# Two hybrid decoder layers on one core: the weight sums of the feed-forward block queued behind the first block's factors, the even half of each up block finished first, and three products opened together in each group

## The chip, the core and the metric

The kernel runs on one core of one Trainium2 chip. The metric is the device time of one execution in microseconds (us), as the median of several runs. The engines are named as the profile names them: PE is TensorE (matmuls and transposes), DVE is VectorE, ACT is ScalarE, POOL is GpSimd, SP is SyncE, which here only issues transfers. Each engine works through its own queue of instructions in order, and waits there for what other engines owe it.

## The reference, cut to what matters

Two decoder layers over 512 tokens with a model width of 1024, all in float32. Around the change only the second half of a layer counts:

```python
x = layer_norm(DN_ALPHA * x + mix, ln1_g, ln1_b)      # after attention
g, u = jnp.split(x @ w_gu, 2, axis=-1)                # w_gu: 1024 x 5632
ffn = (jax.nn.silu(g) * u) @ w_down                   # w_down: 2816 x 1024
ple = (p_i @ w_pp) * jax.nn.sigmoid(x @ w_pg)
return layer_norm(DN_ALPHA * x + ffn + ple, ln2_g, ln2_b)
```

The first half of a layer (a combined input projection, a sliding-window attention, a sparse attention with a top-k per query, an output projection) stays as it is.

## The kernel before, in words

Every float32 matmul is done as three matmuls on a rounded high part and a rest (`mm3`, lines 307 to 311: high by high at line 309, then the two mixed products at 310 and 311). So each weight tile is split: ACT copies the rounded high part (lines 254 and 274) and POOL subtracts to get the rest (lines 255 and 275). The split tiles live in the pool `wsp`, which has five buffers; `w_rel` gives a buffer back and lets the next tile be split. Raw weights arrive by SP's queue in `wst` (three buffers) or, for `w_down`, in `slot` tiles.

The hidden width of 2816 is worked through in eleven *blocks* of 256 columns, and the blocks in *groups* of two: (0, 1), (2, 3), (4, 5), (6, 7), (8, 9), and block 10 alone.

For a block, `gate_up` (line 824) multiplies the transposed activations `fh`/`fl` (all 512 tokens) by four weight tiles: first the two *gate* accumulators, then the two *up* accumulators, one for the first 128 columns of the block (the even half) and one for the last 128 (the odd half), 24 matmuls in each of the four. Every accumulator is one of the eight PSUM buffers with the tag `bank`. In the kernel before, the even and the odd accumulator take turns after every three matmuls. Then ACT applies SiLU to the gates, and DVE multiplies them by the ups (line 849).

For the groups of two blocks, the product with `w_down` is a seven-product (Strassen-Winograd) form over token halves and block halves. It needs sums on both sides:

- `factors` (line 859) makes the sums of the activations on DVE (lines 866, 867, 869, 870) and splits each into high part (ACT, line 855) and rest (DVE, line 856).
- The *weight sums* combine four quarters of `w_down` on DVE: lines 243, 244 and 245 make t1, t2 and t3, each in two instructions of 128x512, and line 259 makes t4 in two more. All operands are in SBUF. In the kernel before, t1 to t3 are written down when the group's raw weights come up in the queue of splits (`w_split`, entry "raw"), and t4 when the first quarter has been split.
- `down` (line 877) does the seven products into six accumulators and adds each result into the residual stream with DVE (`res_out`, line 768, or 770 on the first touch). Some accumulators go on accumulating after they have been added once, so PE can write such a bank again only when DVE has read it.

Nobody writes the order of the instructions by hand here: the kernel is written as one program, and a scheduler with a model of times orders the instructions of each engine, keeping their dependencies. So what is written next to what decides the order only in part, and the order after the change is shown below from the built programs.

After the eleven blocks the layer multiplies the activations by `w_pg` and `p` by `w_pp`, half of their weights split into `slot` tiles by ACT and DVE (lines 268 and 269), and ends with the second layer norm. Before the feed-forward part stands the first layer norm (`ln_sums`, lines 388 to 397) and the transposition of its result (`to_features`, line 399: eight PE transposes at line 405 for each of four token blocks, copied by ACT at 407 and split by DVE at 408).

## Time and profile before

| | |
|---|---|
| median of three runs | 1326.42 us (1325.2 to 1326.89) |
| the profiled execution | 1327.37 us, of which the span from first to last instruction is 1325.6 us |
| PE busy | 1255.6 us, 95% |
| weight loads of PE | 1078.0 us, 81% |
| DVE busy | 854.6 us, 64% |
| POOL busy | 674.4 us, 51% |
| ACT busy | 564.4 us, 43% |
| mean granted TensorE clock | 0.98 |

Times within the profile are counted from the first instruction. The feed-forward parts, with what follows them in the layer, take from 241 to 656 us and from 888 us to the end. In a row of the profile, a number in square brackets is the time for which the engine stood idle just before the instruction, with the engine and the tile that ended the idle time; "x3" means that three equal instructions are put together. PE starts a 128x512 matmul every 0.227 us when nothing holds it, though one such matmul lasts 0.39 us, because they overlap.

### The profile page before, as it was taken

How to read it: one execution, taken by the hardware profiler on the slowest of the kernel's cores; microseconds unless marked ns; L12 is line 12 of the kernel's file. 1: busy time of each engine (PE TensorE's matmuls, PEld its weight loads, DVE VectorE, ACT ScalarE, POOL GpSimd, SP SyncE). 2: the span in 40 equal slices, each digit the busy share in tenths (PEclk: the TensorE clock that was granted, in tenths of full speed). 3: DMA queues.
4: the chain of work that ended last, by engine and by line, in shares of the span. 5: the costliest groups of instructions: out<-in, count | busy, mean ns of one | idle time of the engine just before them, and what ended most of it. 6: DMA issues, size and time to landing. Idle time of an engine off the chain costs nothing.

```text
span 1325.6 us, 18330 instructions
## 1 busy us (share of the span) xinstructions
PE 1255.6 (95%) x6632; PEld 1078.0 (81%) x6632; DVE 854.6 (64%) x1846; ACT 564.4 (43%) x1196; POOL 674.4 (51%) x477
## 2 busy tenths in 40 slices
PE   6799999799999999999998999999999999999996
PEld 4799889687878787887897998978878787878785
DVE  8899965838273737345678998675646464544266
ACT  3657765343333333333336577742424242333220
POOL 7465432356475747572055544323665656656422
PEclk9799999899999999999998999999999999999999
DMA  5133211333233323134032313103241414130421
GB/s 167 49 96 96 80 49 33 96 112 95 80 96 95 103 88 112 48 96 148 1 81 79 113 33 112 48 18 110 96 133 58 143 48 143 52 123 27 121 76 48
DMA packets 89123, 112.77 MB, mean 85 GB/s; under 512 B 5444, under 2 KB 65860, under 8 KB 89032
## 3 DMA queue, kind: packets, MB, share of 16 engines
q1 hardware_dynamic: 88360, 111.58, 27.3%
q8 instruction: 52, 0.85, 0.3%
q14 instruction: 39, 0.32, 0.1%
q10 hardware_dynamic: 672, 0.03, 0.0%
HBM read 109.49 MB, written 2.10 MB: 84 GB/s over the span
## 4 chain that ended last, share of the span: by engine, by line
PE 68%; DVE 24%; issue 3%; ACT 2%; POOL 1%; DMA 1%; DVEq 0%; SPq 0%; POOLq 0%; ACTq 0%
PE bank L309 21%; PE bank L311 20%; PE bank L310 20%; DVE x L768 3%; DVE t2k L243 2%; DVE slot L245 2%; PE bank L649 2%; DVE t2k L469 2%; PE bank L693 2%; DVE m L624 2%; DVE work L625 2%; DVE slot L856 1%; POOL wsp L275 1%; DVE t2k L244 1%; DVE t2k L467 1%
## 5 line engine op out<-in xcount | busy, mean ns | idle before, releaser
L275 POOL TENSOR_TENSOR wsp<-wst,wsp 128x1024 fp32r<-128x1024 f32 (+2 forms) x148 | 364.7, 2478 | 270.0 <-ACT wsp L274 269.7
L310 PE MATMUL bank<-fl,wsp 128*128 128x512 f32 (+1 forms) x768 | 286.8, 374 | 2.0 <-DVE fl L408 2.0
L309 PE MATMUL bank<-fh,wsp 128*128 128x512 f32 (+1 forms) x768 | 285.3, 374 | 1.0 <-ACT fh L407 1.0
L311 PE MATMUL bank<-fh,wsp 128*128 128x512 f32 (+1 forms) x768 | 284.9, 373 | 0.0
L274 ACT CAST wsp<-wst 128x1024 fp32r<-128x1024 f32 (+2 forms) x148 | 151.9, 1032 | 212.2 <-PE bank L311 143.2
L849 DVE TENSOR_TENSOR t2k<-bank,t2k 128x512 f32<-128x512 f32 x44 | 30.0, 691 | 284.3 <-PE bank L311 283.9
L255 POOL TENSOR_TENSOR wsp<-slot,wsp 128x512 fp32r<-128x512 f32 x100 | 135.9, 1383 | 95.6 <-ACT wsp L254 95.6
L309 PE MATMUL bank<-wsp,slot 128*128 128x512 f32 x392 | 156.7, 400 | 15.5 <-DVE x L768 12.1
L310 PEld LDWEIGHTS bank<-fl,wsp 128*128 128x128 f32 x768 | 146.5, 191 | 27.5 <-DVE fl L408 2.4
L309 PEld LDWEIGHTS bank<-fh,wsp 128*128 128x128 f32 x768 | 145.3, 191 | 26.6 <-ACT fh L407 1.9
L311 PEld LDWEIGHTS bank<-fh,wsp 128*128 128x128 f32 x768 | 146.4, 191 | 25.2
L309 PE MATMUL bank<-wsp,fh 128*128 128x256 f32 (+3 forms) x512 | 166.2, 326 | 0.6 <-ACT fh L407 0.2
L311 PE MATMUL bank<-wsp,fl 128*128 128x256 f32 (+3 forms) x512 | 164.9, 323 | 1.6 <-DVE fl L408 1.6
L310 PE MATMUL bank<-wsp,fh 128*128 128x256 f32 (+3 forms) x512 | 164.8, 322 | 0.2 <-POOL wsp L275 0.2
L310 PE MATMUL bank<-wsp,slot 128*128 128x512 f32 x392 | 154.1, 393 | 0.0
L311 PE MATMUL bank<-wsp,slot 128*128 128x512 f32 x392 | 144.9, 393 | 0.0
L768 DVE TENSOR_TENSOR x<-bank,x 128x512 f32<-128x512 f32 x140 | 89.5, 681 | 40.8 <-PE bank L311 40.8
L309 PEld LDWEIGHTS bank<-wsp,fh 128*128 128x128 f32 x512 | 98.4, 193 | 7.4 <-ACT fh L407 0.9
L311 PEld LDWEIGHTS bank<-wsp,fl 128*128 128x128 f32 x512 | 98.3, 192 | 7.2 <-DVE fl L408 2.2
L309 PEld LDWEIGHTS bank<-wsp,slot 128*128 128x128 f32 x392 | 74.3, 190 | 36.6 <-DVE x L768 18.0
L310 PEld LDWEIGHTS bank<-wsp,fh 128*128 128x128 f32 x512 | 98.5, 192 | 6.0 <-POOL wsp L275 0.5
L254 ACT CAST wsp<-slot 128x512 fp32r<-128x512 f32 x100 | 57.1, 618 | 92.1 <-PE bank L311 56.4
(166 smaller groups left out, 2184.2 us busy)
## 6 DMA issues: line engine op xcount, KB each, us to landing
wst<-in_w_gu_dram SPq DMA_DIRECT2D x88, 512.0 KB, 3.5
slot<-in_w_down_dram SPq DMA_DIRECT2D x80, 256.0 KB, 2.8
wst<-in_w_in_dram SPq DMA_DIRECT2D x16, 512.0 KB, 3.7
wst<-in_w_o_dram SPq DMA_DIRECT2D x16, 512.0 KB, 3.7
wst<-in_w_pg_dram SPq DMA_DIRECT2D x16, 512.0 KB, 3.7
wst<-in_w_in_dram SPq DMA_DIRECT2D x8, 256.0 KB, 2.8
lng<-in_ln_g_dram SPq DMA_DIRECT2D x4, 512.0 KB, 4.8
lnb<-in_ln_b_dram SPq DMA_DIRECT2D x4, 512.0 KB, 6.2
```

The source lines that it names most:

```text
L243: V.tensor_tensor(q["t1"][j], q["12"][j], q["11"][j], OP.subtract)
L245: V.tensor_tensor(q["12"][j], q["22"][j], q["12"][j], OP.subtract)
L254: A.copy(w[:, 0, j], src[j])
L255: G.tensor_tensor(w[:, 1, j], src[j], w[:, 0, j], OP.subtract)
L274: A.copy(w[:, 0, :a * n], st[:, :a * n])
L275: G.tensor_tensor(w[:, 1, :a * n], st[:, :a * n], w[:, 0, :a * n], OP.subtract)
L309: PE.matmul(o, sh, mh, start=start, stop=False, skip_group_check=again)
L310: PE.matmul(o, sh, ml, start=False, stop=False, skip_group_check=again)
L311: PE.matmul(o, sl, mh, start=False, stop=stop, skip_group_check=again)
L469: V.tensor_tensor(t1.rearrange("p n (u i) -> p n u i", u=2), t1.rearrange("p n (u i) -> p n u i", u=2), t2.rearrange("p n (u i) -> p n u i ...
L768: V.tensor_tensor(xt[t][:, c], ps, xt[t][:, c], OP.add)
L849: V.tensor_tensor(a, ps[1, f], a, OP.mult)
```

## The change

Four things are rewritten:

1. **The weight sums move.** t1, t2 and t3 are no longer made when the raw quarters come up in the queue of splits, but in a function of their own, `w_sums`, which the driver calls after the first block of the group. `tc.issue_after` tells the scheduler to place them on DVE after a given instruction, here the last split of that block's factors. t4 is tied to the same place.
2. **The up half of a block.** The even accumulator gets all its 24 matmuls first, then the odd one. SiLU, the multiplication and the even part of the factors follow as soon as their half is done. The third weight tile of a block is given back 12 matmuls later than before, since the odd half still needs it.
3. **The factors.** They are made in two steps, one for each half, and the sum for the first split product (s1) is split by itself ahead of the others.
4. **The products.** Three products with six accumulators are opened at the start of a group, instead of two with four accumulators, and each result is added as soon as its product is done.

The amount of arithmetic on PE, ACT and POOL stays the same, except that one split of 128x512 in the factors becomes two of 128x256. The transfers and their order on SP are the same.

```diff
@@ -237,16 +237,9 @@
     def w_split(i):
 
         if wq[i][0] == "raw":
-            q = quarter
-            q["t1"], q["t2"] = ([t2k() for _ in range(2)] for _ in range(2))
-            for j in range(2):
-                V.tensor_tensor(q["t1"][j], q["12"][j], q["11"][j], OP.subtract)
-                V.tensor_tensor(q["t2"][j], q["22"][j], q["t1"][j], OP.subtract)
-                V.tensor_tensor(q["12"][j], q["22"][j], q["12"][j], OP.subtract)
-            q["t3"] = q.pop("12")
             return
         if wq[i][0] == "op":
-            src = quarter.pop(wq[i][1])
+            src = quarter[wq[i][1]]
             wpos["room"] -= 1
...
@@ -255,8 +248,10 @@
                 G.tensor_tensor(w[:, 1, j], src[j], w[:, 0, j], OP.subtract)
             if wq[i][1] == "11":
                 quarter["t4"] = src
-                for j in range(2):
-                    V.tensor_tensor(src[j], quarter["21"][j], quarter["t2"][j], OP.subtract)
+            if wq[i][1] == "t1":
+                with tc.issue_after(quarter["after"]):
+                    for t4, b, t2 in zip(quarter["t4"], quarter["21"], quarter["t2"]):
+                        V.tensor_tensor(t4, b, t2, OP.subtract)
...
@@ -275,6 +270,18 @@
...
+
+    def w_sums(after):
+
+        q = quarter
+        q["after"] = after
+        q["t1"], q["t2"] = ([t2k() for _ in range(2)] for _ in range(2))
+        with tc.issue_after(after):
+            for j in range(2):
+                V.tensor_tensor(q["t1"][j], q["12"][j], q["11"][j], OP.subtract)
+                V.tensor_tensor(q["t2"][j], q["22"][j], q["t1"][j], OP.subtract)
+                V.tensor_tensor(q["12"][j], q["22"][j], q["12"][j], OP.subtract)
+        q["t3"] = q["12"]
 
     def w_pump():
         while True:
@@ -821,58 +828,79 @@
         load_gb(("2", l), ln2_g, ln2_b, l * D)
 
 
-        def gate_up(first):
+        def gate_up(first, made):
+
             ps = {}
             ws = take(4)
+
+            def product(j, f, k, r):
+                wh, wl = (ws[2 * j + k // 4][s][k % 4][:, f * 128:(f + 1) * 128] for s in range(2))
+                mm3(ps[j, f][:, r], wh, wl, fh[:, k, r], fl[:, k, r], k == 0, k == KT - 1)
+
+            def finish(f):
+                a = t2k()
+                A.activation(a, ps[0, f], AF.Silu)
+                V.tensor_tensor(a, ps[1, f], a, OP.mult)
+                made(f, a)
+
             if first:
                 to_features(0)
                 to_features(1)
-            for r in ((0, 256), (256, 512)) if first else ((0, 512),):
                 for j in range(2):
-                    for f in range(2):
-                        if (j, f) not in ps:
-                            ps[j, f] = acc()
+                    ps[j, 0], ps[j, 1] = acc(), acc()
                     for k in range(KT):
-                        wh, wl = (ws[2 * j + k // 4][s][k % 4] for s in range(2))
                         for f in range(2):
-                            fs = slice(f * 128, (f + 1) * 128)
-                            mm3(ps[j, f][:, r[0]:r[1]], wh[:, fs], wl[:, fs],
-                                fh[:, k, r[0]:r[1]], fl[:, k, r[0]:r[1]], k == 0, k == KT - 1)
-                        if r[1] == 512 and k % 4 == 3:
-                            w_rel()
-                    if first and r[0] == 0:
-                        to_features(2 + j)
-            raw = []
+                            product(j, f, k, slice(0, 256))
+                    to_features(2 + j)
+            r = slice(256, 512) if first else slice(0, 512)
             for f in range(2):
-                a = t2k()
-                A.activation(a, ps[0, f], AF.Silu)
-                V.tensor_tensor(a, ps[1, f], a, OP.mult)
-                raw.append(a)
-            return raw
+                if (0, f) not in ps:
+                    ps[0, f] = acc()
+            for k in range(KT):
+                for f in range(2):
+                    product(0, f, k, r)
+                if k % 4 == 3:
+                    w_rel()
+            for f in range(2):
+                if (1, f) not in ps:
+                    ps[1, f] = acc()
+                for k in range(KT):
+                    product(1, f, k, r)
+                    if f == 1 and k % 4 == 3:
+                        w_rel()
+                finish(f)
 
         def parts(src, pair=None):
             h = pair or [slot()[:, :src.shape[1]] for _ in range(2)]
             A.copy(h[0], src)
-            V.tensor_tensor(h[1], src, h[0], OP.subtract)
-            return h
-
-        def factors(raw):
+            end = V.tensor_tensor(h[1], src, h[0], OP.subtract)
+            return h, end.ins
+
+        def factors(r):
 
             lo, hi = slice(0, 256), slice(256, 512)
-            e, o = raw
-            q1, q2 = t2k(), t2k()
-            a11 = slot()
-            r = {"11": parts(e[:, lo], [a11[:, lo], a11[:, hi]])}
-            V.tensor_tensor(q1[:, lo], e[:, hi], o[:, hi], OP.add)
-            V.tensor_tensor(q1[:, hi], q1[:, lo], e[:, lo], OP.subtract)
-            s12 = parts(q1)
-            V.tensor_tensor(q2[:, lo], e[:, lo], e[:, hi], OP.subtract)
-            V.tensor_tensor(q2[:, hi], o[:, lo], q1[:, hi], OP.subtract)
-            odd, s34 = parts(o), parts(q2)
-            for name, src, c in (("s1", s12, lo), ("s2", s12, hi), ("12", odd, lo), ("22", odd, hi),
-                                 ("s3", s34, lo), ("s4", s34, hi)):
-                r[name] = [p[:, c] for p in src]
-            return r
+
+            def made(f, a):
+                r[f] = a
+                if f == 0:
+                    a11 = slot()
+                    r["11"], _ = parts(a[:, lo], [a11[:, lo], a11[:, hi]])
+                    r["q"] = t2k()
+                    V.tensor_tensor(r["q"][:, lo], a[:, lo], a[:, hi], OP.subtract)
+                    return
+                e, o = r.pop(0), r.pop(1)
+                q1, q2 = t2k(), r.pop("q")
+                s12 = [slot(), slot()]
+                V.tensor_tensor(q1[:, lo], e[:, hi], o[:, hi], OP.add)
+                r["s1"], _ = parts(q1[:, lo], [p[:, lo] for p in s12])
+                odd, _ = parts(o)
+                V.tensor_tensor(q1[:, hi], q1[:, lo], e[:, lo], OP.subtract)
+                r["s2"], _ = parts(q1[:, hi], [p[:, hi] for p in s12])
+                V.tensor_tensor(q2[:, hi], o[:, lo], q1[:, hi], OP.subtract)
+                s34, r["end"] = parts(q2)
+                for name, src, c in (("12", odd, lo), ("22", odd, hi), ("s3", s34, lo), ("s4", s34, hi)):
+                    r[name] = [p[:, c] for p in src]
+            return made
 
         def down(hs, first):
 
@@ -891,33 +919,30 @@
                         sh, sl = hs[f][left]
                         mm3(ps[u], sh[:, c], sl[:, c], w[0][f], w[1][f], new and f == 0, stop and f == 1, True)
 
-            pa, pc = [acc(), acc()], [acc(), acc()]
-            w1, w5 = take(2)
+            pa, pc, pb = ([acc(), acc()] for _ in range(3))
+            three = tuple(zip(("11", "s1", "12"), take(3), (pa, pc, pb), ((0, 0), (1, 1), (0, 0))))
             for f in range(2):
-                product("11", w1, pa, (f,), True, True)
-                if f == 1:
-                    w_rel()
-                product("s1", w5, pc, (f,), True, True)
-            w_rel()
-            add(0, 0, pa)
-            add(1, 1, pc)
-            pb = [acc(), acc()]
-            for left, ps, new, out in (("12", pb, True, (0, 0)), ("s2", pa, False, (0, 1)),
-                                       ("s4", pc, False, (0, 1)), ("s3", pa, False, (1, 1)),
-                                       ("22", pa, False, (1, 0))):
+                for left, w, ps, out in three:
+                    product(left, w, ps, (f,), True, True)
+                    if f == 1:
+                        w_rel()
+                        add(*out, ps)
+            for left, ps, out in (("s2", pa, (0, 1)), ("s4", pc, (0, 1)), ("s3", pa, (1, 1)), ("22", pa, (1, 0))):
                 w = w_take()
-                product(left, w, ps, (0, 1), new, True)
+                product(left, w, ps, (0, 1), False, True)
                 w_rel()
                 add(*out, ps)
 
         for gi, fs in enumerate(GROUPS):
             hs = []
             for f in fs:
-                raw = gate_up(f == 0)
                 if len(fs) == 2:
-                    hs.append(factors(raw))
+                    hs.append({})
+                    gate_up(f == 0, factors(hs[-1]))
+                    if f == fs[0]:
+                        w_sums(hs[0]["end"])
                 else:
-                    hs += [parts(a) for a in raw]
+                    gate_up(False, lambda f, a: hs.append(parts(a)[0]))
                 if gi == 1 and f == fs[0]:
                     pT = {}
                     for k in range(2):
```

What this does to the order of DVE at the end of a group, here the third one of the first layer. `x_85` to `x_88` are the four token blocks of the residual stream, `bank` is an accumulator, `slot` a quarter of `w_down` and `t2k` a sum. Before:

```order
L768 TENSOR_TENSOR x_87<-bank,x_87 128x512
L243 TENSOR_TENSOR t2k<-slot 128x512
L768 TENSOR_TENSOR x_88<-bank,x_88 128x512
L768 TENSOR_TENSOR x_85<-bank,x_85 128x512
L768 TENSOR_TENSOR x_86<-bank,x_86 128x512
L768 TENSOR_TENSOR x_85<-bank,x_85 128x512
L244 TENSOR_TENSOR t2k<-slot,t2k 128x512
L245 TENSOR_TENSOR slot<-slot 128x512
L243 TENSOR_TENSOR t2k<-slot 128x512
L768 TENSOR_TENSOR x_86<-bank,x_86 128x512
L768 TENSOR_TENSOR x_85<-bank,x_85 128x512
L244 TENSOR_TENSOR t2k<-slot,t2k 128x512
```

After, the same adds (now line 775) follow each other, with the group's last factor splits (line 876) ahead of them:

```order
L876 TENSOR_TENSOR slot<-t2k,slot 128x512
L775 TENSOR_TENSOR x_85<-bank,x_85 128x512
L775 TENSOR_TENSOR x_86<-bank,x_86 128x512
L775 TENSOR_TENSOR x_87<-bank,x_87 128x512
L775 TENSOR_TENSOR x_88<-bank,x_88 128x512
L775 TENSOR_TENSOR x_85<-bank,x_85 128x512
L775 TENSOR_TENSOR x_86<-bank,x_86 128x512
L775 TENSOR_TENSOR x_85<-bank,x_85 128x512
```

The sums of the next group have left this place. They now stand between the factors of a group's first block and the multiplication (line 843) of its second block:

```order
L876 TENSOR_TENSOR slot<-t2k,slot 128x512
L281 TENSOR_TENSOR t2k<-slot 128x512
L282 TENSOR_TENSOR t2k<-slot,t2k 128x512
L283 TENSOR_TENSOR slot<-slot 128x512
L281 TENSOR_TENSOR t2k<-slot 128x512
L254 TENSOR_TENSOR slot<-slot,t2k 128x512
L282 TENSOR_TENSOR t2k<-slot,t2k 128x512
L283 TENSOR_TENSOR slot<-slot 128x512
L254 TENSOR_TENSOR slot<-slot,t2k 128x512
L843 TENSOR_TENSOR t2k<-bank,t2k 128x512
```

All eight sums of a group stand there one after the other, ahead of everything that the second block needs of DVE.

On PE, the up half of block 10 (its two accumulators have the numbers 5716 and 5717 before) takes turns before:

```order
L309 MATMUL bank_5716<-fh_83,wsp_5611 128x512
L310 MATMUL bank_5716<-fl_84,wsp_5611 128x512
L311 MATMUL bank_5716<-fh_83,wsp_5611 128x512
L309 MATMUL bank_5717<-fh_83,wsp_5611 128x512
L310 MATMUL bank_5717<-fl_84,wsp_5611 128x512
L311 MATMUL bank_5717<-fh_83,wsp_5611 128x512
```

After, the even accumulator (5736) has its 24 matmuls over both weight tiles before the odd one (5768) begins:

```order
L316 MATMUL bank_5736<-fh_83,wsp_5650 128x512
L317 MATMUL bank_5736<-fl_84,wsp_5650 128x512
L318 MATMUL bank_5736<-fh_83,wsp_5650 128x512
L316 MATMUL bank_5768<-fh_83,wsp_5631 128x512
L317 MATMUL bank_5768<-fl_84,wsp_5631 128x512
L318 MATMUL bank_5768<-fh_83,wsp_5631 128x512
```

The same holds in every block. In the groups of two, PE already opened three products at once before the change; their order there is nearly the same as after it.

## The prediction

> **What bounds the kernel now.** I read the page first.
>
> ```profile
> span 1325.6 us, 18330 instructions
> PE 1255.6 (95%) x6632; PEld 1078.0 (81%) x6632; DVE 854.6 (64%) x1846; ACT 564.4 (43%) x1196; POOL 674.4 (51%) x477
> ```
>
> PE is busy for 95% of the span, so the matmuls set the time, and a change that leaves them as they are can only win back time in which PE stands still. So the next view is the list of who waited for whom, for PE (total us, times, longest):
>
> ```profile
> PE bank L309 <- DVE x L768: 12.1, 14, 2.8
> PE bank L610 <- ACT slot L480: 11.7, 2, 6.0
> PE bank L405 <- DVE x L397: 9.4, 3, 5.1
> PE bank L309 <- ACT slot L855: 3.4, 2, 1.7
> ```
>
> Three of these rows lie where the change works. The first: 14 times PE could not write a bank again because DVE had not yet added it into the residual stream. The windows show that these waits come at the ends of groups, and at which ones. Below are the ends of the second and of the fifth group (PE busy, weight loads, DVE, ACT, POOL, granted clock, DMA):
>
> ```profile
> 365.00:395.00 30.00, 28.89 (x126) 23.28 (x125) 24.69 (x29) 10.47 (x15) 21.13 (x12) 1.00 0.31 92
> 559.00:589.00 30.00, 30.00 (x134) 24.86 (x133) 16.26 (x24) 11.42 (x16) 20.27 (x12) 1.00 0.24 71
> ```
>
> At the end of the fifth group PE never stops. That group has the same products, adds and splits, but no pair group follows it, so no weight sums stand among its adds: DVE has 8.4 us less to do. This is a control inside the trace. The timeline shows what the sums do at the end of the third group (DVE rows, then POOL, then PE):
>
> ```profile
> 445.29 0.68 DVE L244 TENSOR_TENSOR t2k<-slot,t2k 128x512 f32<-128x512 f32 x1
> 445.89 2.88 DVE L245 TENSOR_TENSOR slot<-slot 128x512 f32<-128x512 f32 x1
> 448.70 2.88 DVE L243 TENSOR_TENSOR t2k<-slot 128x512 f32<-128x512 f32 x1
> 451.50 1.27 DVE L768 TENSOR_TENSOR x<-bank,x 128x512 f32<-128x512 f32 x2
> ...
> 445.35 8.46 POOL L275 TENSOR_TENSOR wsp<-wst,wsp 128x1024 fp32r<-128x1024 f32 x3
> ...
> 451.28 0.39 PE L311 MATMUL bank<-fh,wsp 128*128 128x512 f32 x1
> 452.23 0.50 PE L309 MATMUL bank<-wsp,slot 128*128 128x512 f32 x1 [0.56 <-DVE x L768]
> 452.56 0.40 PE L310 MATMUL bank<-wsp,slot 128*128 128x512 f32 x1
> ```
>
> A sum takes 0.68 us when it has its way and 2.88 us while POOL splits a tile of 128x1024: two of them hold the queue of DVE for 5.6 us, the add behind them is late, and PE waits for it.
>
> **The change, part by part.** *The adds without the sums.* With the sums gone from the ends of groups, the 12.1 us go, as at the end of the fifth group. Also the last group's 3.4 us:
>
> ```profile
> 604.28 0.50 PE L309 MATMUL bank<-wsp,slot 128*128 128x512 f32 x1 [1.70 <-ACT slot L855]
> ```
>
> Here PE has finished block 10 and needs the high part of its even half. After the change that half is done 24 matmuls earlier, 24 x 0.227 = 5.4 us, against a wait of 1.7. Together 15.5 us in 16 waits.
>
> A wait costs more than its idle time. PE starts matmuls every 0.227 us though each lasts 0.39, so 0.16 is lost before the idle begins, and the first one after it is followed after 0.33 instead of 0.23 (452.23 to 452.56): 0.27 per wait, 16 x 0.27 = 4.3 us. In the first group of each layer the clock goes too:
>
> ```profile
> 325.44 0.50 PE L309 MATMUL bank<-wsp,slot 128*128 128x512 f32 x1 [2.84 <-DVE x L768]
> 327.05 0.63 PE L311 MATMUL bank<-wsp,slot 128*128 128x512 f32 x1
> 327.48 0.63 PE L309 MATMUL bank<-wsp,slot 128*128 128x512 f32 x1
> ...
> 329.19 0.63 PE L310 MATMUL bank<-wsp,slot 128*128 128x512 f32 x1
> ```
>
> For some nine matmuls the step is 0.43 us instead of 0.227, so 9 x 0.20 = 1.8 us, and 3.6 us in two layers. The Trainium skill (TensorE: Matmul & The Clock Gate, Part 1: The HAM clock gate) puts the fall to half the clock behind an idle window of about 3.4 us. By that figure 2.84 us of idle might cost no clock, and the sum would be 3.6 us smaller; the trace shows the slow steps, and I go by the trace.
>
> *The sums leave the layer norm.* The first group's sums stand in the first layer norm now:
>
> ```profile
> 246.45 2.36 DVE L243 TENSOR_TENSOR t2k<-slot 128x512 f32<-128x512 f32 x1
> 249.45 2.69 DVE L395 SCALAR_TENSOR_TENSOR x<-x,lnm,lng 128x1024 f32<-128x1024 f32 x1
> 252.79 0.68 DVE L245 TENSOR_TENSOR slot<-slot 128x512 f32<-128x512 f32 x1
> 256.23 1.28 DVE L397 SCALAR_TENSOR_TENSOR x<-x,lns,lnb 128x1024 f32<-128x1024 f32 x1
> 257.56 1.97 PE L405 MATMUL bank<-idf,x 128*128 128x128 f32 x8 [5.09 <-DVE x L397]
> 904.75 1.09 PE L405 MATMUL bank<-idf,x 128*128 128x128 f32 x8 [2.60 <-DVE x L397]
> ```
>
> Ahead of the L397 at 256.23 stand one sum of 2.3 us and five that advance the queue by 0.6 each: 5.3 us. PE waits 5.09 us for it in the first layer and 2.60 in the second, 7.7 in all. What can come back is a wait for POOL in L395 or L397, which already shows above (L395 takes 2.69 where the other instruction of that size takes 1.28, so 1.4), and up to twice that per layer is conceivable: gain 2.1 to 7.7. I take 7.0, near the upper end, because in the second layer twice as much work leaves as PE waits for.
>
> *Where the sums go.* Eight sums per group now stand on DVE ahead of everything of the second block, and so of its factors, of which PE needs the first early in the products. Durations before (min/median/max):
>
> ```profile
> L243 DVE TENSOR_TENSOR t2k<-slot x20: 678/1800/2884, 246.4 to 1158.4; 128x512 f32<-128x512 f32 x20
> L244 DVE TENSOR_TENSOR t2k<-slot,t2k x20: 676/679/2296, 252.2 to 1162.4; 128x512 f32<-128x512 f32 x20
> L245 DVE TENSOR_TENSOR slot<-slot x20: 677/1486/2891, 252.8 to 1164.0; 128x512 f32<-128x512 f32 x20
> L259 DVE TENSOR_TENSOR slot<-slot,t2k x20: 676/679/682, 284.8 to 1191.4; 128x512 f32<-128x512 f32 x20
> ```
>
> A block is 96 x 0.227 = 21.8 us of PE. The first block's factors end about 5 us into the second block: after the two multiplications they take 434.14 to 440.02 in the rows below, 5.9 us, less what the even half now does earlier, plus a multiplication. The even half of the second block can be multiplied at 72 x 0.227 = 16.3 us, so 11.3 us are free. PE reads the first factor of that half 18 matmuls into the products, at 25.9; the multiplication, copy and split ahead of it need 2 to 3 us, so the sums may last until about 22.8, that is 17.8 us, before PE waits. Eight sums at these medians are 2 x (1.80 + 0.68 + 1.49 + 0.68) = 9.3 us. Bounds: 5.4 us at the minimum, 23.1 at 2.89 each. I take the medians, since POOL has less to do there than where the sums stand now (the fifth busy time; the first window is the second block of the third group, the other the end of that group):
>
> ```profile
> 411.00:433.00 22.00, 22.00 (x99) 18.22 (x98) 10.71 (x13) 7.53 (x14) 10.80 (x8) 1.00 0.22 72
> 433.00:455.00 22.00, 21.44 (x95) 17.41 (x94) 21.94 (x26) 9.40 (x14) 16.81 (x9) 1.00 0.32 96
> ```
>
> So this costs nothing, covered by 17.8 us of matmuls. ACT and POOL wait for t1 when they split it, and behind it stand t2 and later tiles; the first product with t1 starts 23.2 us into the block, 8.9 us after the sums end by this reckoning (5 + 9.3 = 14.3). The Trainium skill (SBUF — State Buffer, SBUF: two separate sides) says that a DVE instruction with two SBUF inputs and a POOL instruction exclude each other for their whole length; the rows at 445.35 agree, and by it the upper bound is what eight unlucky sums would cost (the third rival).
>
> *Products and banks.* PE opened three products already, so six accumulators at once bring nothing and cost nothing. The third weight tile of a block comes back 12 matmuls, 2.7 us, later. The tile that takes its buffer is used five tiles on, over 20 us later, and POOL is idle for half of the second block (10.80 busy of 22 above): no cost taken, up to 2.7 us for a block without that cover. The extra split in the factors is 2 x 0.41 for 0.68 us on DVE, under the same cover.
>
> *Giving back.* The part with `w_pg` begins 2 us earlier after block 10, while its weights come by transfers and splits that do not get faster:
>
> ```profile
> L309 PE MATMUL bank<-slot,fh 128*128 128x512 f32 x64 | 24.9, 389 | 0.0
> wst<-in_w_pg_dram SPq DMA_DIRECT2D x16, 512.0 KB, 3.7
> ```
>
> Now PE waits 0.0 there. Between 0 and all that the last group gains (3.4 + 2 x 0.27 = 3.9) may return; I take 1.0. For short new waits at the ends of groups I take another 1.0 (0 to 9.9, the first rival). The scheduler also orders the second layer's attention anew, with the same work; PE has a wait of 6.0 there (L610 above), and I allow half of it, 3, either way and take nothing.
>
> Sum: 15.5 + 4.3 + 3.6 + 7.0 - 1.0 - 1.0 = 28.4 us. The profiled execution took 1327.37 us with a span of 1325.6; the median of the runs is 1326.42. So I forecast a span of 1297.2 and a median of **1298.0 us**; with the bounds of the layer norm and the attention 1293 to 1304.
>
> **The rivals.** *The factors hold the adds.* Without the sums, DVE still does factor sums on SBUF operands right ahead of the adds, and POOL splits at the same time:
>
> ```profile
> 434.14 1.52 DVE L866 TENSOR_TENSOR t2k<-t2k 128x256 f32<-128x256 f32 x1
> 435.59 1.50 DVE L869 TENSOR_TENSOR t2k<-t2k 128x256 f32<-128x256 f32 x1
> 438.12 1.90 DVE L856 TENSOR_TENSOR slot<-t2k,slot 128x512 fp32r<-128x512 f32 x3
> 439.93 1.88 DVE L768 TENSOR_TENSOR x<-bank,x 128x512 f32<-128x512 f32 x3
> ```
>
> If more of them are held, the twelve short waits stay: 12 x (0.55 + 0.27) = 9.9 us, so 1298.0 + 9.9 - 1.0 = 1307. Against it: the fifth group has these factors and no wait.
>
> *Later parts give it back.* The `w_pg` weights return 3.9 instead of 1.0, and the attention's new order costs its 3: 1298 + 2.9 + 3 = 1304. For it speaks the 3.7 us of each transfer; against it the 0.0.
>
> *The sums hold the second block (slower).* If each of the eight sums waits for one POOL instruction and takes 2.89, they last 23.1 us instead of 17.8, and PE waits 5.3 us in each of ten groups: 53 us, 1298 + 53 = 1351. It decides from 2.58 us per sum on, where ten waits of 2.84 eat the 28.4. Against it: no kind of sum has a median over 1.80, and POOL idles half of that time.
>
> *It moves without effect.* PE's waits go over to another releaser, such as the splits of POOL with the later third tile, and the time stays near 1326. POOL's 51% and the fifth group speak against it.
>
> **How the numbers follow.** Forecast 0.74, factors 0.10, later parts 0.08, slower 0.05, no effect 0.03. The range of 1291 to 1309 takes in the forecast with its own range, the first two rivals, and 2 us below 1293 for more than the full gain in the layer norm. A measurement of this kernel can tell about 0.2% from no change, 2.7 us. Faster by more: the first three and a share of the last, 0.93; within: 0.02; slower: 0.05.
>
> **What would show it.** Right: in PE's waits the rows "L309 <- DVE x" and "L309 <- ACT slot" are gone or under 2 us, the wait for the layer norm is under 3 us, windows at the ends of all groups show PE busy throughout, and the first group's matmuls keep the step of 0.227. The sums stand between a first block's last split and the second block's multiplication, with a median under 1.8 us. Wrong: new idle of PE ahead of a product's second half, released by ACT or DVE factors (the sums hold), ahead of adds (the factors hold), or in the part with `w_pg`.

## The result, and the profile after

The changed kernel takes 1296.59 us in the median of four runs (1295.42 to 1298.64), the kernel before 1326.66 us beside it. The ratio is 0.977, with a 95% interval of 0.975 to 0.979. The forecast was 1298.0 us. The profiled execution of the changed kernel took 1295.42 us, with a span of 1293.6 us against 1325.6 before: 32.0 us less.

The line numbers have moved by some lines: the products stand at 316 to 318 (309 to 311 before), the adds at 775 and 777 (768 and 770), the layer norm at 402 and 404 (395 and 397), the transposes at 412 (405), and the sums at 281 to 283 and 254 (243 to 245 and 259). First the page of the changed kernel, its span and engines, and then the list of who waited for whom, for PE (total us, times, longest):

```profile
span 1293.6 us, 18329 instructions
PE 1244.4 (96%) x6632; PEld 1073.3 (83%) x6632; DVE 837.7 (65%) x1866; ACT 575.7 (44%) x1216; POOL 666.8 (52%) x477
```

```profile
PE bank L617 <- ACT slot L487: 11.6, 2, 5.9
...
PE bank L412 <- DVE x L404: 4.2, 4, 1.7
...
PE bank L700 <- ACT t2k L720: 2.1, 1, 2.1
```

The rows for the adds (12.1 us in 14 waits) and for block 10's high part (3.4 in 2) have no answer in this list: they are gone. For the layer norm the row has fallen from 9.4 to 4.2, but the two rows do not hold the same waits. In both kernels the transposes of the second token block wait 1.7 us in each layer. The row of before counts one of these two waits (the other stands in the list under another releaser), the row of after counts both. The waits ahead of the third block's transposes, in which the sums had a part, fell from 7.7 us (5.09 and 2.60) to 0.8. The row of L700, in the second layer's attention, is new. The windows at the ends of groups confirm it. These are the second and the fifth group (PE busy, weight loads, DVE, ACT, POOL, granted clock, DMA):

```profile
355.00:385.00 30.00, 30.00 (x134) 24.86 (x133) 14.92 (x22) 12.75 (x18) 22.18 (x14) 1.00 0.35 106
548.00:578.00 30.00, 30.00 (x134) 24.83 (x133) 12.40 (x19) 11.68 (x15) 22.00 (x12) 1.00 0.34 102
```

PE never stops at either. DVE is busy for 14.9 us at the end of the second group, where it was 24.7: the sums have left. They stand where the change put them. Below are the four kinds of sums (shortest, median and longest in ns, with the first and last start in us), and the first and last sum of the third group:

```profile
L281 DVE TENSOR_TENSOR t2k<-slot x20: 679/684/1785, 280.2 to 1163.1; 128x512 f32<-128x512 f32 x20
L282 DVE TENSOR_TENSOR t2k<-slot,t2k x20: 677/686/1520, 280.9 to 1165.5; 128x512 f32<-128x512 f32 x20
L283 DVE TENSOR_TENSOR slot<-slot x20: 676/1230/1790, 281.5 to 1166.1; 128x512 f32<-128x512 f32 x20
L254 DVE TENSOR_TENSOR slot<-slot,t2k x20: 677/1226/1778, 283.8 to 1167.8; 128x512 f32<-128x512 f32 x20
```

```profile
404.35 0.68 DVE L281 TENSOR_TENSOR t2k<-slot 128x512 f32<-128x512 f32 x1
...
410.89 1.77 DVE L254 TENSOR_TENSOR slot<-slot,t2k 128x512 f32<-128x512 f32 x1
```

The eight last 8.3 us (404.35 to 412.66). A sum never takes 2.88 us any more: in this stretch POOL works on pieces of 128x512, and a held sum lasts 1.5 to 1.8.

In the layer norm the idle time fell, and so did the time around it. The transposes of the third token block in each layer, which stood at [5.09 ...] and [2.60 ...] before, now read:

```profile
252.65 1.09 PE L412 MATMUL bank<-idf,x 128*128 128x128 f32 x8 [0.39 <-DVE x L404]
884.40 1.09 PE L412 MATMUL bank<-idf,x 128*128 128x128 f32 x8 [0.40 <-DVE x L404]
```

So 4.7 and 2.2 us of idle went, 6.9 together. But from the first to the fourth block's transposes the part shortened from 25.0 to 18.4 us in layer 1 and from 23.2 to 18.4 in layer 2, 11.3 us. The rest is clock. These windows of the kernel before lie behind the 5.09 us of waiting in layer 1 and at the start of the layer norm of layer 2 (the granted clock is the first number behind POOL's):

```profile
256.00:266.00 10.00, 8.44 (x56) 8.44 (x57) 4.88 (x11) 1.17 (x2) 0.00 (x0) 0.73 0.16 66
...
888.00:903.00 15.00, 11.21 (x66) 10.24 (x64) 15.00 (x26) 4.87 (x10) 10.25 (x4) 0.77 0.56 169
```

And the changed kernel in the same places:

```profile
253.00:260.00 7.00, 7.00 (x62) 7.00 (x61) 3.21 (x7) 1.11 (x3) 0.00 (x0) 1.00 0.66 218
872.00:884.00 12.00, 9.05 (x68) 8.00 (x66) 12.00 (x25) 5.31 (x10) 11.26 (x4) 1.00 0.41 132
```

The clock was 0.73 and 0.77 there, and is 1.00 now.

The time by stages, for this and all later kernels, is read from PE's rows: a feed-forward part runs from the first transpose after the first layer norm to the first transpose of the next layer (or to the last matmul), the layer norm's share of it to the fourth block's transposes, and the second layer's attention lies between. In us:

| kernel | layer norm 1 | feed-forward 1 | attention 2 | layer norm 2 | feed-forward 2 | ratio to before |
|---|---|---|---|---|---|---|
| before | 25.0 | 415.1 | 232.1 | 23.2 | 427.1 | 1 |
| changed | 18.4 | 397.2 | 234.6 | 18.4 | 410.7 | 0.977 |
| sums_only | 18.4 | 398.8 | 232.0 | 20.2 | 414.3 | 0.977 |
| last_block | 18.4 | 397.1 | 234.5 | 18.4 | 410.7 | 0.977 |
| two_products | 18.4 | 397.0 | 234.5 | 18.4 | 410.8 | 0.976 |
| unpinned | 18.4 | 397.0 | 234.7 | 18.4 | 410.7 | 0.976 |
| first_group | 18.4 | 408.6 | 231.7 | 20.5 | 424.3 | 0.993 |
| no_sums | 18.4 | 398.8 | 231.5 | 20.4 | 414.5 | 0.979 |
| sums_early | 24.7 | 421.7 | 236.5 | 23.2 | 432.3 | 1.011 |
| dose16 | 18.4 | 403.3 | 234.8 | 18.4 | 417.0 | 0.987 |
| dose24 | 18.4 | 427.9 | 234.5 | 18.4 | 441.6 | 1.024 |
| before_split_512 | 24.5 | 406.5 | 233.6 | 25.2 | 419.4 | 0.987 |
| split_512 | 16.8 | 395.3 | 234.3 | 16.8 | 409.5 | 0.972 |
| split_256 | 16.2 | 395.1 | 232.4 | 16.2 | 409.1 | 0.975 |

### The profile page after: what moved, and what is told of

The parts are those of the page before. It is cut to its first block, busy times and chain, and to the rows that moved or that the text cites. A ratio compares the mean times of both kernels' runs of the same rounds, so it can differ in the third digit from the quotient of the medians.

```text
span 1293.6 us, 18329 instructions
## 1 busy us (share of the span) xinstructions
PE 1244.4 (96%) x6632; PEld 1073.3 (83%) x6632; DVE 837.7 (65%) x1866; ACT 575.7 (44%) x1216; POOL 666.8 (52%) x477
## 4 chain that ended last, share of the span: by engine, by line
PE 81%; DVE 12%; ACT 2%; issue 2%; DMA 1%; POOL 1%; DVEq 0%; SPq 0%; POOLq 0%; ACTq 0%
PE bank L316 24%; PE bank L317 24%; PE bank L318 24%; PE bank L656 2%; PE bank L700 2%; DVE t2k L476 2%; PE bank L694 2%; DVE work L620 1%; DVE m L631 1%; DVE work L632 1%; DVE t2k L474 1%; DMA wst<-in_w_pg_dram 1%; DVE x L404 1%; POOL wsp L270 1%; PE bank L486 1%
## 5 line engine op out<-in xcount | busy, mean ns | idle before, releaser
L270 POOL TENSOR_TENSOR wsp<-wst,wsp 128x1024 fp32r<-128x1024 f32 (+2 forms) x148 | 353.4, 2402 | 273.4 <-ACT wsp L269 271.2
L316 PEld LDWEIGHTS bank<-fh,wsp 128*128 128x128 f32 x768 | 143.6, 188 | 26.6 <-ACT fh L414 1.9
L318 PEld LDWEIGHTS bank<-fh,wsp 128*128 128x128 f32 x768 | 144.7, 188 | 24.9
L248 POOL TENSOR_TENSOR wsp<-slot,wsp 128x512 fp32r<-128x512 f32 x100 | 141.5, 1439 | 28.5 <-ACT wsp L247 28.5
L875 ACT CAST slot<-t2k 128x256 fp32r<-128x256 f32 (+1 forms) x104 | 49.8, 497 | 144.1 <-DVE t2k L843 102.5
L248 POOL TENSOR_TENSOR wsp<-t2k,wsp 128x512 fp32r<-128x512 f32 x40 | 57.5, 1448 | 93.0 <-ACT wsp L247 93.0
```

Of the source, the lines that this page charges most:

```text
L248: G.tensor_tensor(w[:, 1, j], src[j], w[:, 0, j], OP.subtract)
L270: G.tensor_tensor(w[:, 1, :a * n], st[:, :a * n], w[:, 0, :a * n], OP.subtract)
L316: PE.matmul(o, sh, mh, start=start, stop=False, skip_group_check=again)
L318: PE.matmul(o, sl, mh, start=False, stop=stop, skip_group_check=again)
L875: A.copy(h[0], src)
```

## The experiments

The theory was that the gain comes from the sums leaving two places, the adds and the layer norm. The first rival was that the new order of halves, factors and products earns most of it.

**Only the sums moved** (sums_only). The kernel before, with the sums behind the first block's last split:

```diff
 hs.append(factors(raw))
+if f == fs[0]:
+    w_sums(ends[-1])        # ends: the splits of the factors, in order
```

> The kernel before with one part of the change: the weight sums are made behind the first block's last split. Order of the halves, factors and the two opening products are the old ones. Theory: all of the gain but that of the last group, 3.9 us: 1300.5 us, 1297 to 1304. Rival (the new order of halves, factors and products earns most of it): 1315 or more.

It took 1298.19 us (1297.93 to 1299.76), 0.977 of the kernel before (0.976 to 0.979). The rival wanted 1315 or more and is out. The waits for adds are gone, while block 10's wait is still in the list:

```profile
PE bank L316 <- ACT slot L864: 3.4, 2, 1.7
```

The table gives the price of sums among the adds. Outside the layer norm, feed-forward 1 went from 390.1 to 380.3 us and feed-forward 2 from 403.9 to 394.1: 19.6 us together.

**The sums among the adds again** (sums_early). The changed kernel, with the sums written down where the raw quarters are loaded, without the tie:

```diff
     SP.dma_start(quarter[q][j], w[r:r + 128, h * 512:(h + 1) * 512])
+w_sums()
...
-        w_sums(hs[0]["end"])
```

> The changed kernel with the weight sums written down where their raw quarters are loaded and without the tie to the factors, so that six of the eight sums of each group stand on DVE among the previous group's adds again, and in the first layer norm for the first group; the new order of the halves, the factors and the three products stay. Theory (the gain is that the sums leave the adds and the layer norm): it loses the 12.1 us of waits for adds, 14 x 0.27 of restarts, 3.6 us of clock in the first groups and the 11.4 us by which the layer-norm part got shorter between the two traces, 30.9 in all, so about 1327 us, 1318 to 1328. Rival (the new order of halves, factors and products earns most of it): 1297 to 1310.

It took 1343.07 us (1341.62 to 1345.09), a ratio of 1.011 (1.010 to 1.012): slower than the kernel before. The direction is the theory's, but the size is beyond both forecasts. Outside the layer norm it loses 35 us in two layers where 19.5 were expected. The list shows fewer and longer waits than before, and the timeline what follows each of them:

```profile
PE bank L313 <- DVE x L772: 22.3, 8, 3.2
```

```profile
326.25 0.80 PE L313 MATMUL bank<-wsp,slot 128*128 128x512 f32 x1 [3.16 <-DVE x L772]
326.85 0.63 PE L314 MATMUL bank<-wsp,slot 128*128 128x512 f32 x1
327.27 0.63 PE L315 MATMUL bank<-wsp,slot 128*128 128x512 f32 x1
...
331.11 0.63 PE L315 MATMUL bank<-wsp,slot 128*128 128x512 f32 x1
```

Eight waits of 2.65 to 3.16 us, one at the end of each of the four groups in a layer that pair sums follow, instead of 14 of which twelve were short. Behind six of the eight, 5 to 12 matmuls step at 0.43 us instead of 0.227. So 22.3 us are idle, 8 x 0.27 = 2.2 are restarts, and of the 10.7 that remain the 44 slow steps make 8.8, at 0.20 each. With the rest of the change in place, the sums do more harm among the adds than without it. They hold DVE no longer: at the end of the third group two held sums take 5.6 us (450.81 to 456.39), as in the kernel before (445.89 to 451.50). But PE runs out of matmuls 3.6 us after the first of the two begins, not 5.8 us. That this comes from the new order of products is likely, but was not tried by itself.

**The opening of three products** (two_products). The changed kernel with the old opening:

```diff
-pa, pc, pb = ([acc(), acc()] for _ in range(3))
+pa, pc = [acc(), acc()], [acc(), acc()]
+w1, w5 = take(2)
...
+pb = [acc(), acc()]
```

> The changed kernel with the old opening of a group: two products with four accumulators, then the third. Theory: opening three brings nothing and costs nothing, 1296.6 within 2.7 us. Rival: six accumulators spare PE waits for adds at the start of a group's products: 0.82 us (0.55 idle and 0.27 of restart) in each of ten groups, so 1304 or more.

It took 1297.20 us (1295.01 to 1298.20), and both feed-forward parts agree with those of the changed kernel to 0.2 us. The third product opened early is worth nothing that these runs can tell.

**The tie to the last split** (unpinned). The changed kernel, with the sums written down in the queue of splits as before:

```diff
 if wq[i][0] == "raw":
+    q = quarter
...
+    for j in range(2):
+        V.tensor_tensor(q["t1"][j], q["12"][j], q["11"][j], OP.subtract)
...
     return
...
-        w_sums(hs[0]["end"])
```

> The changed kernel without the tie of the sums to the last split: they are written down where the raw quarters come up in the queue of splits, and the scheduler puts six of them into the even half's factors of a group's first block, ahead of the odd half's multiplication, and t4 into the odd half's factors. Theory: it only matters that they are out of the adds and out of the layer norm; nothing of PE needs the first block's factors for another block of 21.8 us, so 1296.6 within 3 us. Rival: the place behind the last split is what counts; the odd half's multiplication comes late by the sums, 6 x 1.3 = 7.8 us, and holds its banks against the next block: from 1 us in each of ten groups on, so 1306 or more.

It took 1297.05 us (1295.17 to 1297.42); the feed-forward parts are 397.0 and 410.7 us. Some sums were held for longer than in the changed kernel, and delayed nobody:

```profile
396.94 2.84 DVE L244 TENSOR_TENSOR t2k<-slot,t2k 128x512 f32<-128x512 f32 x1
```

So the place behind the last split is not what counts. With the rest of the change in place the scheduler moves the sums out of the adds and the layer norm even without the tie. In the new order of halves the third weight tile comes back later, and with it the queue of splits comes later to the raw quarters; that this is the reason was not tried by itself.

**The even half of block 10 alone** (last_block). sums_only, with the even half finished first in the last block:

```diff
-raw = gate_up(f == 0)
+raw = gate_up(f == 0, len(fs) == 1)     # halves one after the other, each split at once
```

> The kernel before with the weight sums moved, and with the even half finished first in block 10 alone; all other blocks, the factors and the opening of two products are the old ones. Against the kernel before on the same chip the sums alone were 0.9774. Theory (of the other parts only the even half of block 10 earns, and what they lose is in the second layer's attention, 234.6 us against 232.0): the 3.4 us of waits before block 10's second half and 2 x 0.27 go, so 3.9 us less than the sums alone, ratio 0.9745, about 1294 where the kernel before takes 1327.5; 5 us less than that if the attention stays at 232.0. Rival: the wait comes back later, in the part with w_pg, whose weights come no earlier: ratio 0.977.

It took 1296.80 us (1295.06 to 1297.21), 0.977 of the kernel before (0.975 to 0.978). The interval holds the rival's number and not quite the theory's; the stages say more than the total. Outside the layer norm the feed-forward parts get 1.6 and 1.8 us shorter than in sums_only: block 10's wait, at its idle time. The times of all stages are then those of the changed kernel, so nothing is left for the order of halves in blocks 0 to 9, the factors in two steps and the third product. With this edit alone the attention went from 232.0 to 234.5 us, and this row appeared, as in the changed kernel:

```profile
PE bank L700 <- ACT t2k L720: 2.1, 1, 2.1
```

With POOL's pieces uncut, the four kernels that keep the old order of block 10 took 231.5 to 232.1 us for the second layer's attention, and those with the new one 234.5 to 234.8, or 236.5 (sums_early). Most of it comes back at once. The layer norm that follows takes 20.2 us in sums_only and 18.4 in last_block, and the difference is clock. So an edit in block 10 re-ordered the attention of the next layer, with effects as large as some terms of the forecast. First the window of sums_only, then that of last_block:

```profile
868.00:883.00 15.00, 12.32 (x63) 10.88 (x62) 14.46 (x30) 8.28 (x16) 12.22 (x4) 0.77 0.34 107
```

```profile
868.00:883.00 15.00, 12.05 (x81) 10.58 (x80) 14.38 (x32) 8.86 (x16) 12.26 (x4) 1.00 0.35 105
```

**The sums of the first group alone** (first_group). The kernel before, with the sums moved in group 0 and left among the adds in the others:

```diff
 if wq[i][0] == "raw":
+    if wq[i][2] != 0:
+        w_sums(None)
     return
...
+                    if f == 0:
+                        w_sums(ends[-1])
```

> The kernel before with the sums moved for the first group of each layer alone; the other groups' sums stay among the adds. Theory (the sums in the layer norm cost their idle time and the clock after it): the layer-norm parts get 11.4 us shorter in two layers, as between the two traces, so 11.4 us faster than the kernel before. Rival (idle alone counts, the 7.0 us of the prediction, or 5.2 us as the rows of waits fell): 5 to 7 us faster.

It took 1319.20 us (1317.43 to 1320.02), 0.993 of the kernel before (0.992 to 0.995), 8.8 us faster. Between the two forecasts: the layer norm went from 25.0 to 18.4 and from 23.2 to 20.5 us, 9.3 together, of which 7.3 are idle (4.7 and 2.6) and the rest is clock, nearly all of it in layer 1. The other 2.0 us, up to the 11.3 that the traces differ by, are the clock of 0.77 in layer 2, which this kernel keeps:

```profile
880.00:895.00 15.00, 12.05 (x62) 10.73 (x62) 14.52 (x29) 7.88 (x14) 12.22 (x4) 0.77 0.34 108
```

So those 2.0 us do not come from the sums. They went in the kernels with the other order of the attention. What that order shifts is where PE's idle time lies in the intervals of 3.41 us at whose ends the granted clock changes (the last section works this out). In sums_only one such interval holds 1.95 us of idle time, the wait of 1.7 us for the second block's transposes among it, and the clock falls behind it:

```profile
872.35:875.77 3.42, 1.47 (x12) 0.99 (x10) 3.42 (x8) 1.68 (x4) 3.42 (x2) 1.00 0.39 116
875.77:879.18 3.41, 2.68 (x11) 2.39 (x12) 3.41 (x7) 2.71 (x6) 3.41 (x3) 0.50 0.52 174
```

In last_block the wait is as long, but no interval holds more than 1.72 us, and the clock stays up:

```profile
872.00:875.41 3.41, 1.69 (x13) 1.33 (x13) 3.41 (x3) 1.53 (x3) 3.41 (x2) 1.00 0.06 14
875.41:878.83 3.42, 2.19 (x17) 1.74 (x16) 3.42 (x12) 3.10 (x7) 3.42 (x2) 1.00 0.56 163
```

So these 2.0 us hang on where an interval begins. Each kernel was traced in one execution, so whether it falls out like this every time is not shown.

**No sums at all** (no_sums). The kernel before, with the products taking raw quarters in place of the sums:

```diff
-src = quarter.pop(wq[i][1])
+src = quarter[{"t1": "12", "t2": "22", "t3": "12", "t4": "11"}.get(wq[i][1], wq[i][1])]
```

> The kernel before with all weight sums left out: the products use the raw quarters in their place, so a part of the computation is missing and the time is a bound for what moving the sums can bring. Order of halves, factors and products are the old ones, so it is to be compared with the kernel in which only the sums moved (0.9774 of the kernel before). Theory (where the sums stand now they are covered wholly): the same within 0.2%, 0.975 to 0.979. Rival (they still cost some tenths of a us in each of ten groups, by short waits or by holding ACT's and POOL's splits): 0.974 or less.

It took 1298.76 us (1297.65 to 1300.45), 0.979 of the kernel before (0.977 to 0.981). Feed-forward 1 takes 398.8 us, as in sums_only; feed-forward 2 takes 414.5 against 414.3. Where the sums stand now, they cost nothing that the stages show, and the move has brought all that a move of them can bring.

**More sums** (dose16, dose24). The changed kernel with 8 and with 16 extra sums in each group:

```diff
 V.tensor_tensor(q["t2"][j], q["22"][j], q["t1"][j], OP.subtract)
+for _ in range(4):          # 8 in dose24
+    V.tensor_tensor(q["t2"][j], q["22"][j], q["t1"][j], OP.subtract)
```

> The changed kernel with eight extra sums per group (t2 made anew four times in each half), so that 16 instead of 8 stand between the first block's factors and the second block's multiplication. In the changed kernel eight took 8.3 us in the first group (280.2 to 288.5), so 16 should take 14 to 20. Theory (17.8 us of cover, as PE needs the second block's first factor only in the products): 0 to 2 us per group past the cover, in ten groups 0 to 20, so 1297 to 1317, near the lower end. Rival (cover ends where the second block's even half can be multiplied, 11.3 us): 3 to 8 us in each of ten groups, 1327 or more.

> The changed kernel with sixteen extra sums per group, 24 in all. With 16 they lasted 14.3 us (409.74 to 424.13) in a group, and PE lost 1.24 us per group, at the adds behind the second block's factors. At 0.68 each for most, 24 should last 19 to 21 us. Theory (from some 13 us on DVE has no slack left up to the adds, so each further us of sums delays the first add by one): 5 to 7 us more per group, 1296.6 + 10 x (6.2 to 8.2), 1359 to 1379. Rival (the cover of 17.8 us from the prediction, up to the second block's first factor, with only short waits before): 2 to 3 us per group past it and the 1.24, 1329 to 1340.

dose16 took 1310.00 us (1309.54 to 1310.19), dose24 1359.10 us (1357.52 to 1360.57). Against the changed kernel the feed-forward parts got 12.4 and 61.6 us longer, 1.24 and 6.2 us for each of ten groups. In dose16 the sums of the third group last from 409.74 to 424.13, 14.4 us. No product waits for a factor's high part there. In the first group of each layer PE waits once for a factor's rest (0.70 us), and in every group DVE comes late to the adds behind the second block's factors:

```profile
434.33 0.50 PE L318 MATMUL bank<-wsp,slot 128*128 128x512 f32 x1 [0.60 <-DVE x L777]
```

In dose24 the sums reach past the second block's multiplication, and PE waits for the first factor, first for its high part and then for its rest:

```profile
PE bank L318 <- ACT slot L877: 22.1, 10, 3.0
...
PE bank L320 <- DVE slot L878: 8.9, 12, 1.2
```

```profile
442.95 0.50 PE L318 MATMUL bank<-wsp,slot 128*128 128x512 f32 x1 [2.03 <-ACT slot L877]
...
445.35 1.22 PE L320 MATMUL bank<-wsp,slot 128*128 128x512 f32 x2 [0.87 <-DVE slot L878]
446.38 0.63 PE L318 MATMUL bank<-wsp,slot 128*128 128x512 f32 x1
...
449.79 0.63 PE L320 MATMUL bank<-wsp,slot 128*128 128x512 f32 x1
```

The two rows of waits make 3.1 us per group; restarts and the matmuls at half pace make up the rest of the 6.2. The forecast for dose24, that the adds are delayed by each further us, gave the right total by the wrong wait.

**POOL's pieces cut** (before_split_512, split_512, split_256). In the kernel before, and in the changed kernel, POOL's subtraction for a weight tile is cut into pieces:

```diff
-G.tensor_tensor(w[:, 1, :a * n], st[:, :a * n], w[:, 0, :a * n], OP.subtract)
+for c in range(0, a * n, 512):          # 256 in split_256
+    c = slice(c, min(c + 512, a * n))
+    G.tensor_tensor(w[:, 1, c], st[:, c], w[:, 0, c], OP.subtract)
```

> The kernel before, sums among the adds and in the layer norm as they were, with one thing changed: POOL's subtraction of a weight tile is cut into pieces of 512 columns. Theory (a sum holds DVE's queue because it waits for POOL's running instruction, 2.4 us for 128x1024): a held sum lasts at most about 1.8 us instead of 2.88, as in the rows of the changed kernel where POOL's pieces are of 512 columns; two held sums in a row take 3.6 instead of 5.6, so most of the 14 waits of PE for an add get 2 us shorter, which leaves under 3 of the 12.1 us and no slow clock after them, and the layer norm shortens as well: 12 to 20 us faster than the kernel before. Rival (it is the number of instructions ahead of the adds, not what each waits for): the 5 us that the same cut earned on the changed kernel, 3 to 7 us faster.

before_split_512 took 1310.33 us (1309.59 to 1310.61), 0.987 of the kernel before (0.986 to 0.989), 16 us faster with every sum still among the adds and in the layer norm. The end of the third group, with the sums between the adds as before:

```profile
436.45 0.68 DVE L244 TENSOR_TENSOR t2k<-slot,t2k 128x512 f32<-128x512 f32 x1
437.05 1.77 DVE L245 TENSOR_TENSOR slot<-slot 128x512 f32<-128x512 f32 x1
438.75 1.78 DVE L243 TENSOR_TENSOR t2k<-slot 128x512 f32<-128x512 f32 x1
440.45 1.28 DVE L770 TENSOR_TENSOR x<-bank,x 128x512 f32<-128x512 f32 x2
```

Two held sums take 3.4 us instead of 5.6, and the add is in time: PE's row of waits for adds is gone, and the feed-forward parts outside the layer norm take 382.0 and 394.2 us, near the 380.3 and 394.1 of sums_only; the 1.7 us more in layer 1 are a stretch of 3.41 us at half clock behind block 10's wait. So the length of POOL's running instruction is what made the sums harmful. The layer norm did not follow:

```profile
PE bank L407 <- DVE x L399: 12.2, 2, 6.1
```

There four of the six sums were held, for 1.4 to 1.8 us each, where one of 2.36 us was before, and PE waits 6.1 us in place of 5.09.

> The changed kernel with POOL's subtraction of a weight tile cut into pieces of 512 columns, so that a DVE instruction on two SBUF operands waits for at most about 1.2 us instead of 2.4. Theory (what is left of the layer norm's waits, 4.2 us, and of the 0.69 to 1.79 of a sum, is a wait for POOL's running instruction): 1 to 4 us faster than the changed kernel, and DVE's busy time falls by some 20 us. Rival: each piece pays its own start on POOL (148 tiles, some 0.1 to 0.3 us each, by nothing measured here), PE then waits for weight tiles in the first blocks, no gain or 1 to 3 us slower.

split_512 took 1291.38 us (1290.06 to 1292.37), 0.972 of the kernel before (0.971 to 0.974), below the interval of the changed kernel. The layer norm takes 16.8 us instead of 18.4 in each layer, and POOL is busy for 694 us instead of 667, for which nobody waits. By stages 3.4 us of the gain lie from the first layer norm on, within the 1 to 4 expected, and 1.9 us in the first layer's attention. DVE's busy time fell by 9 us, not 20. It is the fastest version of these runs.

> The changed kernel with POOL's subtraction of a weight tile cut into pieces of 256 columns. Pieces of 512 columns gave 0.9724 of the kernel before (the changed kernel 0.9773): the layer-norm part fell from 18.43 to 16.75 us in each layer, and the pieces cost POOL 27 us more. Theory (DVE's instructions wait for the running piece): a little more of the layer norm, 0.5 us in each layer, and another 30 to 60 us of POOL that nobody waits for, 0.970 to 0.973. Rival (POOL's added time holds weight tiles): 0.974 or more.

split_256 took 1293.05 us (1292.51 to 1293.85), 0.975 (0.973 to 0.976), which is the rival's number and not the theory's. From the first layer norm on it is 2.4 us faster than split_512, 16.2 us of layer norm included, but the first layer's attention ends 4.6 us later (its first transpose behind it at 243.58 us against 239.01). Not all of that is the cut's. two_products and the changed kernel have the same order of instructions up to that transpose, and yet it comes at 243.11 us in one and at 240.90 in the other: from 27.9 to 31.3 us the granted clock is 0.50 in two_products and 1.00 in the changed kernel. In split_256 it is 0.51 there, in split_512 1.00. So what the finer cut itself costs in the attention, and whether PE waits there for weight tiles as the rival has it, stays open.

## Why the prediction was right

The forecast sum was 28.4 us and the span fell by 32.0. Term by term:

| term of the prediction | forecast | measured | by |
|---|---|---|---|
| adds without the sums (12.1, 14 restarts of 0.27, clock 3.6) | 19.5 | 19.6 | sums_only against before |
| block 10 (3.4, 2 restarts), less 1.0 given back | 2.9 | 3.4 | last_block against sums_only |
| sums out of the layer norm | 7.0 | 9.3 | first_group against before |
| short new waits at the ends of groups | -1.0 | 0 | windows, list of waits |
| attention of layer 2 in another order | 0 | -2.5 | last_block against sums_only |
| clock in the second layer norm | none | 2.0 | first_group against changed |
| sum | 28.4 | 31.8 | |

- **The adds.** The step was right in place and size, and sums_only shows that the move of the sums alone earns it. before_split_512 shows the cause that the prediction read off the timeline, a sum held by POOL's long instruction. The count of 0.27 per restart and 0.20 per slow step made 7.4 of the 19.5 us; the idle time alone would have been over a third too low.
- **The layer norm.** This is the term that was mis-sized. "I take 7.0" was a bet on idle time, and 6.9 us of idle went (4.7 and 2.2). But the clock that the prediction had counted after a wait of 2.84 us, among the adds, it did not count after the wait of 5.09 us here, although the row with eight transposes in 1.97 us instead of 1.09 was quoted. The window with 0.73 shows this clock, 1.9 us in layer 1 by first_group. The 0.77 in layer 2 is another matter: it stays when the sums leave, so its 2.0 us belong to no term of the prediction.
- **Block 10 and the part with w_pg.** 3.9 less 1.0 was taken, and 3.4 measured: half as much was given back as taken. The row of the products on w_pg reads 0.1 us of idle after the change.

```profile
L317 PE MATMUL bank<-slot,fh 128*128 128x512 f32 x64 | 25.1, 392 | 0.1
```

- **What should cost nothing.** Three opened products, the third weight tile's later return, the extra split: two_products and last_block leave 0.2 us for all of it, as forecast.
- **The cover.** "Eight sums at these medians are 9.3 us": they took 8.3, and no_sums shows no cost.
- **The slower rival.** It did not happen, but its price was wrong. It put the point of decision at 17.8 us of sums and let the second block's first factor be the first to come late. dose16 shows that in four of a layer's five groups the adds come late first, at 14.4 us of sums already, for 1.24 us per group on average. And beyond the point the price was taken as idle time alone; dose24 shows 6.2 us per group, of which 3.1 are the waits.
- **The other rivals.** The factors do not hold the adds with eight sums; with sixteen they begin to. Later parts gave back 0.5 instead of 3.9, and the attention its 2.5 of 3. As a case of its own this rival was half right.
- **Luck.** The mechanism held, but that the sum came within 3.6 us is in part luck. The attention's 2.5 us of loss and the 2.0 us of clock in the second layer norm stand in no term, and they nearly cancel.
- **Two slips in the working.** 12 x (0.55 + 0.27) is 9.8, not 9.9. And with the stated bounds of the layer norm (2.1 to 7.7) and of the attention (3 either way) the forecast runs from 1294.3 to 1305.9, not from 1293 to 1304. Neither changes the outcome.

## What to carry to other kernels

Where an instruction takes several times its usual duration, look for what it waits for on another engine, and ask which end is cheaper to change: here cutting POOL's instruction in two earned half of what moving DVE's work did, and added to it. Price a stall of the matmul engine with what stands behind it in the trace, the restart and the steps at half pace, at every wait that is long enough and not only at the first one noticed. Whether the clock falls is read from the engine's idle time per interval of the clock's grid, not from the length of one wait. Before a move is built, the same kernel without the moved work gives the most that it can bring, and extra copies of the moved work show how much room the new place has.

## What the runs showed of the hardware

- **The clock is halved behind an interval of 3.41 us in which PE stood idle for half of it.** Within each trace the changes of the granted clock lie whole multiples of 3.41 us apart. In the feed-forward parts of the fourteen traces there are 31 such intervals at full clock in which PE's idle time sums up to 1.79 us or more, and behind each of them the clock is 0.50. It did not fall behind any with 1.72 us or less, among them 53 with over 1.0 us. In the attention, where PE runs short matmuls, the line is less sharp. So a wait costs clock by its length and by how it lies on this grid. In sums_early six of eight waits of 2.65 to 3.16 us were followed by half pace, and two of 2.67 by none. The first two lines below are about a wait of 2.67 us of which 2.33 lie in one interval; the other three are about one of the same length, which a boundary parts so that the two intervals hold 1.48 and 1.18 us of idle time (PE busy first, the granted clock behind POOL):

```profile
454.79:458.21 3.42, 1.09 (x5) 0.91 (x6) 3.42 (x4) 0.00 (x0) 3.42 (x2) 1.00 0.67 217
458.21:461.62 3.41, 3.41 (x10) 2.63 (x9) 3.41 (x5) 1.04 (x1) 1.76 (x2) 0.50 0.66 213
...
519.65:523.06 3.41, 1.93 (x9) 1.27 (x7) 3.41 (x2) 0.80 (x1) 3.41 (x3) 1.00 0.44 147
523.06:526.48 3.42, 2.24 (x10) 1.83 (x11) 3.42 (x5) 0.48 (x1) 2.77 (x1) 1.00 0.54 165
526.48:529.89 3.41, 3.41 (x17) 2.81 (x16) 2.30 (x4) 0.57 (x1) 2.40 (x1) 1.00 0.48 154
```

  In the same way, block 10's wait in before_split_512 cost clock in layer 1 (1.79 us, all in one interval) and none in layer 2 (1.78 us, with 1.53 us of idle time in the fuller interval). The Trainium skill (TensorE: Matmul & The Clock Gate, Part 1: The HAM clock gate) puts the fall behind an idle window of about 3.4 us; here half of such a window was enough, so the measurement decides.
- **A DVE instruction on two SBUF operands waits for POOL's running piece, so the piece's length sets the wait.** The same 128x512 sum took 0.68 us alone, up to 1.79 against POOL pieces of 128x512 and 2.88 against pieces of 128x1024. The Trainium skill (SBUF — State Buffer, SBUF: two separate sides) says that the two exclude each other for their whole length, and the rows agree. Cutting POOL's piece costs POOL little. The splits of the 148 weight tiles took 353 us whole and 379 us in 296 pieces, 0.17 us for each added piece. First the row of the changed kernel, then that of split_512 (busy us, mean ns, idle before):

```profile
L270 POOL TENSOR_TENSOR wsp<-wst,wsp 128x1024 fp32r<-128x1024 f32 (+2 forms) x148 | 353.4, 2402 | 273.4 <-ACT wsp L269 271.2
```

```profile
L272 POOL TENSOR_TENSOR wsp<-wst,wsp 128x512 fp32r<-128x512 f32 (+2 forms) x296 | 378.9, 1311 | 258.3 <-ACT wsp L269 234.4 <-issue 23.3 <-POOL slot L482 0.5
```
